# Placing activation tiles against weight tiles in SBUF: new offsets modulo 512 bytes for the squared MLP values, the normed activations and the mixer outputs

## The chip, the cores and the metric

The kernel runs on one core of one Trainium2 chip. The metric is the device time of one execution in microseconds (us); smaller is better. A measurement of a kernel is the median of several runs.

## The reference: what is computed

One layer of a hybrid decoder block on 256 tokens of 2048 features, in float32:

```python
n = rmsnorm(h, g_mix);  z = n @ w_in;  q, k, v, u = split(z)
a = moba_attention(q, k, v, dist_bias)           # 8 heads of 128, one causal block here
c = conformer_conv(u, ...)                       # gate, 31-tap depthwise conv, layernorm, silu
h = h + concat([a, c]) @ w_out
h = h + cross_attention(rmsnorm(h), rmsnorm(mem), wq, wk, wv, wo)
nm = rmsnorm(h, g_mlp)
h = h + square(relu(nm @ w1)) @ w2               # d_ff = 8192
return rmsnorm(h, g_final)
```

The weights are 200 pieces of 1 MiB. Of them 128 belong to the MLP (64 to `w1`, 64 to `w2`).

## The kernel before

**Three matmuls for one.** Every float32 operand of a large product is split in two float32r tiles, a high part H and a low part L, so that a product becomes three matmuls that add into one PSUM bank: high by high, high by low, low by high (`mm3`, line 102, which calls `mm`, line 98; the matmul itself is line 99). Each matmul names a *stationary* operand of 128x128, which a weight load (LDWEIGHTS, on the profile's PEld rows) puts into the array, and a *moving* operand of 128 x N columns, which streams through it. The weight load of the next matmul runs while the present matmul streams.

**The weight steps.** A loop over 200 steps (line 911) handles one 1 MiB piece each. SyncE loads the piece into one of 4 `raw` buffers (line 119, four steps ahead), ScalarE copies its high part into `wh` (line 158) and VectorE subtracts to get the low part `wl` (line 170; in some steps GpSimd, line 168), two steps ahead, into rings of 3 buffers each. TensorE then runs the step's matmuls. The steps are, in order: U 0 to 15, V 16 to 23, QK 24 to 39, MK and MV 40 to 47 (keys and values of the memory), Wout 48 to 63, Wq 64 to 67, Wo 68 to 71, and the MLP from 72: four times 16 steps of W1 and 16 steps of W2. The order of instructions on each engine is the order in which the program is written.

**Two forms of a step.** In `weight_stationary` (line 280; U, QK, MK, Wout, W1; Wq and Wo have the same roles) the weight tiles are stationary and the activations move, 256 columns at a time: 48 matmuls in a step, stationary wh, wh, wl, moving H, L, H. In `act_stationary` (line 293; V, MV, W2) the activations are stationary and the weights move, 512 columns at a time: 24 matmuls in a step, stationary H, H, L, moving wh, wl, wh. Four consecutive steps of a block go through four groups of activations, one group per step.

**The activation tiles.** `act_tiles` holds four groups, each a pair actH, actL of 4 x 256 columns: the normed input of a product (groups 0 to 3, `split_act`, line 181). The eight tiles tagged `mixH`/`mixL` with a0, a1, c0, c1 hold first the mixer outputs (a: attention, c: convolution; they feed Wout), then the cross-attention output (a0, feeds Wo), and in the MLP the squared values sH, sL of block b (`evac_w1`, line 789; they feed W2). For Wo, the tiles of a1 and c0 hold one split piece of weights at their start (`wo_split0`, line 714).

**Where the tiles stand.** `shifted` (line 174) allocates 4*256+32 words and uses 4*256 of them, starting `shift` words in (`ACT_SHIFT`, line 42; `MIX_SHIFT`, line 43). Tiles follow each other in SBUF in the order of first use, so their places depend on the sizes of all before them; the first is the scratch of `dynamic_dma_scratch_size` bytes (line 1017; DMAs here are all issued by SyncE). A row of a stationary operand is 512 bytes and each moving operand is a multiple of 1024, so all parts of one tile have the same byte address modulo 512. In the built program these places are:

| tile | before, address modulo 512 | activation minus weights, modulo 256 (H, L) |
|---|---|---|
| wh, wl (all 6 buffers) | 384 | |
| act group 0: H, L | 192, 320 | (64, 192) |
| act group 1: H, L | 448, 64 | (64, 192) |
| act group 2: H, L | 320, 448 | (192, 64) |
| act group 3: H, L | 64, 192 | (192, 64) |
| a0, also s of block 0: H, L | 0, 128 | (128, 0) |
| a1, also s of block 1: H, L | 256, 384 | (128, 0) |
| c0, also s of block 2: H, L | 256, 0 | (128, 128) |
| c1, also s of block 3: H, L | 384, 128 | (0, 0) |

The last column is worked out from the one before it. It is called the *offset* of a group below.

Of the kernel before, what the change touches and what calls it, by code (L numbers as in the profile page):

```python
# [10 lines left out]
F32R = mybir.dt.float32r  # L11
# [4 lines left out]
P = 128  # L16
T = 256
# [21 lines left out]
WOUT_ORDER = [(0, 0), (1, 0), (2, 0), (0, 1), (1, 1), (2, 1), (3, 0), (3, 1)]  # L39
STEP_US = 5.25  # L40

ACT_SHIFT = (16, 16, 16, 16)
MIX_SHIFT = {"a0": 0, "a1": 0, "c0": 0, "c1": 0}


def bucket(d):
# [29 lines left out]
def tile_hybrid_block(ctx: ExitStack, tc: tile.TileContext, xT, memT, w, par, rel, gfin, out):  # L76
    nc = tc.nc
    act, dve, pool, pe = nc.scalar, Metered(nc.vector), nc.gpsimd, nc.tensor
    ctx.enter_context(tc.manual_schedule())
    sb = ctx.enter_context(tc.tile_pool(name="sb", bufs=1))  # L80
# [4 lines left out]
    def nm(s):  # L85
        count[0] += 1
        return f"{s}_{count[0]}"

    def ring(shape=(P, 512)):
        return sb.tile(list(shape), F32, tag="ring", name=nm("ring"), bufs=7)  # L90
# [81 lines left out]
    act_tiles = {}  # L172

    def shifted(tag, shift, name=None):
        t = sb.tile([P, 4 * T + 32], F32R, tag=tag, name=nm(name or tag))
        return t[:, shift:shift + 4 * T].rearrange("p (a b) -> p a b", a=4)

    def new_act(g):
        act_tiles[g] = tuple(shifted(f"act{x}{g}", ACT_SHIFT[g]) for x in "HL")

    def split_act(g, src, gain, i):
        hi, lo = act_tiles[g]
# [5 lines left out]
    def split_act_group(g, src, gain):  # L188
        new_act(g)
        for i in range(4):  # L190
            split_act(g, src, gain, i)
# [54 lines left out]
    def twice(rb):  # L246
        return rb.unsqueeze(1).to_broadcast([P, 2, T])

    def pair(ap):
        return ap.rearrange("p (a b) -> p a b", a=2)  # L250
# [73 lines left out]
    def split_both(j, g):  # L324
        new_act(g)
        split_tiles(j)
        for i in range(4):
            s = slice(i * 512, (i + 1) * 512)
            split_act(g, hT[g], G_MIX, i)
            act.activation(wh[j][:, s], raw[j][:, s], AF.Copy)  # L330
            dve.tensor_sub(wl[j][:, s], raw[j][:, s], wh[j].bitcast(F32)[:, s])
# [69 lines left out]
    MIX = ["a0", "a1", "c0", "c1"]  # L401
# [35 lines left out]
    mix = {}  # L437

    def mix_tiles(key):
        if key not in mix:  # L440
            mix[key] = tuple(shifted(f"mix{x}{key}", MIX_SHIFT[key]) for x in "HL")
        return mix[key]

    def evac_split(dst, i, src):
# [4 lines left out]
    def self_attention(b):  # L449
# [56 lines left out]
        def evac_o():  # L506
            for h in heads:
                evac_split(mix_tiles(MIX[h // 4]), h % 4, st["o", h])
# [70 lines left out]
    def ln_silu(i):  # L579
        sg, z = ln[i]  # L580
        dve.tensor_tensor(z, z, sg, op=OP.mult)
        hi, lo = mix_tiles(MIX[2 + i // 2])
        s = slice(2 * (i % 2), 2 * (i % 2) + 2)
        act.activation(hi[:, s, :], z, AF.Copy)
        dve.tensor_sub(lo[:, s, :], z, hi.bitcast(F32)[:, s, :])
# [108 lines left out]
    def cx_e(h):  # L694
        if not cx_o:
            mix.clear()
            cx_o.append(mix_tiles("a0"))
        evac_split(cx_o[0], h, cx["o", h])
# [85 lines left out]
    sT = {}  # L784
# [2 lines left out]
    gb = []  # L787

    def evac_w1(b, banks):
        sT[b] = tuple(shifted(f"mix{x}{MIX[b]}", MIX_SHIFT[MIX[b]], f"s{x}{b}") for x in "HL")  # L790
        for n in range(2):
            y, s = ring((P, 2, T)), ring((P, 2, T))
            d = slice(2 * n, 2 * n + 2)
            dve.scalar_tensor_tensor(y, pair(banks[n].ap), 0.0, twice(RB["2"]), op0=OP.max, op1=OP.mult)
            act.activation(s, y, AF.Square)
            act.activation(sT[b][0][:, d, :], y, AF.Square)  # L796
            dve.tensor_sub(sT[b][1][:, d, :], s, sT[b][0].bitcast(F32)[:, d, :])
# [60 lines left out]
    for q in range(4):  # L858
        j0 = MLP0 + 32 * q
        for b in range(4):  # L860
            block(j0 + 4 * b, 4, weight_stationary, act_pair, lambda bk, b=b: evac_w1(b, bk),
                  lag=2 if q == b == 0 else 0)
# [164 lines left out]
```

## Time and profile before

| | us |
|---|---|
| median of 3 runs | 1190.11 (1188.60 to 1190.23) |
| the profiled execution's own time | 1188.36 |
| its span, first to last instruction | 1186.6 |
| TensorE busy in the span | 1160.6 |
| VectorE busy | 707.8 |
| ScalarE busy | 540.8 |
| granted TensorE clock, mean | 0.993 of full speed |

The profile is one execution on the chip. Its engines are PE (matmuls), PEld (weight loads), DVE (VectorE), ACT (ScalarE), POOL (GpSimd) and SP (SyncE, here the DMA queue). A matmul's row gives its start and a duration in which the next one has already begun, since matmuls are pipelined; what a matmul costs is therefore the distance from its start to the start of the next one, here called its *pitch*. Windows are given in us from the start of the span.

### The profile page before, as it was taken

How to read it: one execution, taken by the hardware profiler on the slowest of the kernel's cores; microseconds unless marked ns; L12 is line 12 of the kernel's file. 1: busy time of each engine (PE TensorE's matmuls, PEld its weight loads, DVE VectorE, ACT ScalarE, POOL GpSimd, SP SyncE). 2: the span in 40 equal slices, each digit the busy share in tenths (PEclk: the TensorE clock that was granted, in tenths of full speed). 3: DMA queues.
4: the chain of work that ended last, by engine and by line, in shares of the span. 5: the costliest groups of instructions: out<-in, count | busy, mean ns of one | idle time of the engine just before them, and what ended most of it. 6: DMA issues, size and time to landing. Idle time of an engine off the chain costs nothing.

```text
span 1186.6 us, 18443 instructions
## 1 busy us (share of the span) xinstructions
PE 1160.6 (98%) x7976; PEld 1076.4 (91%) x7976; DVE 707.8 (60%) x821; ACT 540.8 (46%) x564; POOL 113.6 (10%) x100
## 2 busy tenths in 40 slices
PE   7969999999999999999999999999999999999996
PEld 7969899999999999999888999888999888999885
DVE  6659998787666668555444545454455454445443
ACT  7535344465666456554333344333444333444342
POOL 3243121012003003000000000000000000000112
PEclk9989999999999999999999999999999999999999
DMA  9766554444554534545655544555554655554532
GB/s 353 247 195 217 187 205 172 154 145 175 185 190 165 199 115 178 197 159 195 231 183 204 181 178 177 213 178 191 197 180 156 218 194 180 189 199 146 213 139 71
DMA packets 35000, 221.02 MB, mean 186 GB/s; under 512 B 3816, under 2 KB 6504, under 8 KB 9448
## 3 DMA queue, kind: packets, MB, share of 16 engines
q1 hardware_dynamic: 34920, 219.86, 52.5%
q8 instruction: 62, 1.02, 0.3%
q14 instruction: 18, 0.15, 0.0%
HBM read 216.18 MB, written 3.67 MB: 185 GB/s over the span
## 4 chain that ended last, share of the span: by engine, by line
PE 92%; DMA 4%; DVE 2%; ACT 1%; issue 0%; SPq 0%; ACTq 0%; DVEq 0%
PE mm L99 86%; PE cv L99 4%; DMA dram_rev<-ring 3%; PE sm L99 2%; DMA raw<-in_w_dram 1%; DVE wl L65 1%; DVE cv L65 1%; ACT wh L158 0%; PE sm L808 0%; PE sm L494 0%; PE sm L684 0%; SPq L129 0%; SPq L128 0%; DVE acc L65 0%; ACT ring L841 0%
## 5 line engine op out<-in xcount | busy, mean ns | idle before, releaser
L65 DVE TENSOR_TENSOR wl<-raw,wh 128x2048 fp32r<-128x2048 f32 (+1 forms) x205 | 447.0, 2187 | 316.0 <-ACT wh L158 313.4
L158 ACT ACTIVATE wh<-raw 128x2048 fp32r<-128x2048 f32 x195 | 373.5, 1915 | 531.6 <-PE mm L99 421.6
L99 PE MATMUL mm<-actH,wh 128*128 128x256 f32 x1600 | 453.1, 283 | 14.1 <-ACT wh L158 8.0
L99 PE MATMUL mm<-actH,wl 128*128 128x256 f32 x1600 | 450.8, 282 | 1.8 <-DVE wl L65 1.8
L99 PE MATMUL mm<-actL,wh 128*128 128x256 f32 x1600 | 450.3, 281 | 0.0
L99 PEld LDWEIGHTS mm<-actH,wh 128*128 128x128 f32 x1600 | 302.8, 189 | 14.7 <-ACT wh L158 8.2
L99 PEld LDWEIGHTS mm<-actH,wl 128*128 128x128 f32 x1600 | 303.3, 190 | 2.5 <-DVE wl L65 2.5
L99 PEld LDWEIGHTS mm<-actL,wh 128*128 128x128 f32 x1600 | 303.1, 189 | 0.3
L99 PE MATMUL mm<-wh,sL 128*128 128x512 f32 x512 | 202.2, 395 | 0.0
L99 PE MATMUL mm<-wl,sH 128*128 128x512 f32 x512 | 201.4, 393 | 0.0
L99 PE MATMUL mm<-wh,sH 128*128 128x512 f32 x512 | 201.4, 393 | 0.0
L99 PEld LDWEIGHTS mm<-wl,sH 128*128 128x128 f32 x512 | 96.3, 188 | 22.9
L99 PEld LDWEIGHTS mm<-wh,sL 128*128 128x128 f32 x512 | 96.2, 188 | 22.3
L99 PEld LDWEIGHTS mm<-wh,sH 128*128 128x128 f32 x512 | 96.2, 188 | 22.0
L65 DVE SCALAR_TENSOR_TENSOR cv<-hp,part,cv 128x256 f32<-128x256 f32 x240 | 97.7, 479 | 0.0
L892 POOL TENSOR_TENSOR acc<-acc,gb 128x512 f32<-128x512 f32 x6 | 12.1, 2041 | 677.5 <-ACT ring L828 677.5
L65 DVE TENSOR_TENSOR sL<-ring,sH 128x512 fp32r<-128x512 f32 x32 | 22.2, 692 | 67.0 <-ACT sH L796 67.0
L209 POOL TENSOR_TENSOR acc<-acc,ring 128x512 f32<-128x512 f32 x17 | 35.5, 2088 | 168.2 <-ACT ring L208 167.4
L168 POOL TENSOR_TENSOR wl<-raw,wh 128x512 fp32r<-128x512 f32 x24 | 32.4, 1382 | 99.1 <-ACT wh L158 99.1
L99 PE MATMUL mm<-wh,actH 128*128 128x512 f32 x96 | 38.2, 398 | 0.0
L99 PE MATMUL mm<-wh,actL 128*128 128x512 f32 x96 | 37.9, 395 | 0.0
L99 PE MATMUL mm<-wl,actH 128*128 128x512 f32 x96 | 37.9, 394 | 0.0
(156 smaller groups left out, 1042.3 us busy)
## 6 DMA issues: line engine op xcount, KB each, us to landing
raw<-in_w_dram SPq DMA_DIRECT2D x199, 1024.0 KB, 4.8
mem<-in_memT_dram SPq DMA_DIRECT2D x4, 512.0 KB, 7.0
out_dram<-acc SPq DMA_DIRECT2D x8, 256.0 KB, 3.1
hT<-in_xT_dram SPq DMA_DIRECT2D x3, 512.0 KB, 7.4
dram_rev<-ring SPq DMA_DIRECT2D x1, 1532.0 KB
raw<-in_w_dram SPq DMA_DIRECT2D x4, 256.0 KB, 3.9
bias<-dram_rev SPq DMA_DIRECT2D x1, 1024.0 KB, 5.8
gb<-in_gfin_dram SPq DMA_DIRECT2D x4, 256.0 KB, 7.2
```

The costliest lines, as they stand in the source:

```text
L65: return op(out, *args, **kw)
L99: pe.matmul(o, lhsT=lhsT, rhs=rhs, start=not bk.begun, stop=stop, skip_group_check=True)
L158: act.activation(wh[j], raw[j], AF.Copy)
L168: pool.tensor_sub(wl[j][:, s], raw[j][:, s], wh[j].bitcast(F32)[:, s])
L209: eng.tensor_tensor(self.acc, self.acc, sq, op=OP.add)
L892: pool.tensor_mul(d, d, gb[cb])
```

## The change

The room around an activation tile grows from 32 to 128 words, each of the 16 tiles has a shift of its own, and the DMA scratch shrinks from 8192 to 1024 bytes, which moves all tiles. The mixer outputs and the squared values, which share tiles, now differ by 16 words (64 bytes). No instruction is added, removed, resized or moved on any engine; only operand addresses differ.

```diff
-ACT_SHIFT = (16, 16, 16, 16)
-MIX_SHIFT = {"a0": 0, "a1": 0, "c0": 0, "c1": 0}
+ROOM = 128
+ACT_SHIFT = {"H0": 16, "H1": 16, "H2": 112, "H3": 112, "L0": 16, "L1": 16, "L2": 112, "L3": 112}
+S_SHIFT = {"Ha0": 32, "Ha1": 32, "Hc0": 96, "Hc1": 96, "La0": 32, "La1": 32, "Lc0": 96, "Lc1": 96}
+MIX_STEP = 16
...
-        t = sb.tile([P, 4 * T + 32], F32R, tag=tag, name=nm(name or tag))
+        t = sb.tile([P, 4 * T + ROOM], F32R, tag=tag, name=nm(name or tag))
...
-        act_tiles[g] = tuple(shifted(f"act{x}{g}", ACT_SHIFT[g]) for x in "HL")
+        act_tiles[g] = tuple(shifted(f"act{x}{g}", ACT_SHIFT[f"{x}{g}"]) for x in "HL")
...
-            mix[key] = tuple(shifted(f"mix{x}{key}", MIX_SHIFT[key]) for x in "HL")
+            mix[key] = tuple(shifted(f"mix{x}{key}", (S_SHIFT[x + key] + MIX_STEP) % ROOM) for x in "HL")
...
-        sT[b] = tuple(shifted(f"mix{x}{MIX[b]}", MIX_SHIFT[MIX[b]], f"s{x}{b}") for x in "HL")
+        sT[b] = tuple(shifted(f"mix{x}{MIX[b]}", S_SHIFT[x + MIX[b]], f"s{x}{b}") for x in "HL")
...
-    nc = bacc.Bacc("TRN2", target_bir_lowering=False, num_devices=1, dynamic_dma_scratch_size=8192)
+    nc = bacc.Bacc("TRN2", target_bir_lowering=False, num_devices=1, dynamic_dma_scratch_size=1024)
```

The places in the built program after it:

| tile | after, address modulo 512 | offset (H, L) |
|---|---|---|
| wh, wl (all 6 buffers) | 128 | |
| all act groups: H, L | 192, 192 | (64, 64) |
| mixer outputs and cross-attention output: H, L | 192, 192 | (64, 64) |
| squared values s of all blocks: H, L | 128, 128 | (0, 0) |

The one split piece of Wo in a1 and c0 stands at 0 and 256 after the change (before: 256 and 384 in a1, 256 and 0 in c0).

## The prediction

> **What bounds the kernel now.** I read the page first: which engine is busy, and what the chain that ended last is made of.
>
> ```profile
> span 1186.6 us, 18443 instructions
> PE 1160.6 (98%) x7976; PEld 1076.4 (91%) x7976; DVE 707.8 (60%) x821; ACT 540.8 (46%) x564; POOL 113.6 (10%) x100
> PE 92%; DMA 4%; DVE 2%; ACT 1%; issue 0%; SPq 0%; ACTq 0%; DVEq 0%
> ```
>
> TensorE is busy 98% of the span and is 92% of the chain. The next question is where it waits. The view of waits, for TensorE, gives four rows for the first 113.6 us (the two largest below) and none for the rest.
>
> ```profile
> PE mm L99 <- ACT wh L158: 8.0, 1, 8.0
> PE mm L99 <- ACT wh L330: 6.1, 1, 6.1
> ```
>
> So from 113.6 us on, time is the sum of the matmuls' pitches. The busy time of stretches shows it, and shows what the other engines have left (columns: window, its length, then busy us and count of PE, PEld, DVE, ACT, POOL, then granted clock, DMA share, GB/s):
>
> ```profile
> 113.58:158.48 44.90, 44.90 (x197) 36.25 (x195) 44.27 (x81) 20.36 (x18) 8.25 (x8) 1.00 0.53 188
> 158.48:181.00 22.52, 22.52 (x193) 22.52 (x192) 21.53 (x34) 8.82 (x6) 6.57 (x4) 1.00 0.52 191
> 181.00:284.56 103.56, 103.56 (x859) 102.73 (x857) 82.13 (x168) 57.10 (x97) 12.97 (x9) 1.00 0.46 163
> 549.72:638.75 89.03, 89.03 (x386) 72.17 (x385) 43.27 (x27) 32.85 (x20) 0.00 (x0) 1.00 0.57 201
> 638.75:729.06 90.31, 90.31 (x770) 90.30 (x768) 45.57 (x31) 37.24 (x28) 0.00 (x0) 1.00 0.53 187
> 729.06:818.10 89.04, 89.04 (x386) 72.17 (x385) 43.29 (x27) 32.86 (x20) 0.00 (x0) 1.00 0.54 189
> 908.40:997.45 89.05, 89.05 (x387) 72.18 (x385) 43.30 (x27) 32.85 (x20) 0.00 (x0) 1.00 0.54 189
> 1087.75:1176.60 88.85, 88.85 (x386) 71.98 (x384) 41.33 (x38) 35.25 (x37) 13.61 (x8) 1.00 0.37 131
> ```
>
> The rows of 89 us are the four runs of W2 (384 matmuls of 512 columns each), the row of 90.31 is one run of W1 (768 matmuls of 256 columns). PE is busy for the whole of each, at full clock, and in the MLP nothing else exceeds 57%. The exception is 113.58 to 181.00 (V and the first QK block): DVE is busy 44.27 of 44.90 us and 21.53 of 22.52 us there, so matmuls that got shorter would soon wait for `wl`.
>
> **What addresses cost in the trace of before.** The change touches only addresses, and before happens to hold five different offsets, in steps of equal work. I cut windows at the steps of W2, blocks 0 to 3 of one cycle, then at W1, groups 0 to 3, at Wout (a0, a1, c0, c1), and at V, groups 1 and 2.
>
> ```profile
> 571.96:577.57 5.61, 5.61 (x25) 1.00 0.61 197
> 577.57:583.17 5.60, 5.60 (x25) 1.00 0.59 196
> 583.17:588.75 5.58, 5.58 (x25) 1.00 0.53 185
> 588.75:594.23 5.48, 5.48 (x26) 1.00 0.52 187
> ...
> 638.76:644.37 5.61, 5.61 (x49) 1.00 0.53 187
> 644.37:649.99 5.62, 5.62 (x50) 1.00 0.54 191
> 649.99:655.64 5.65, 5.65 (x50) 1.00 0.54 187
> 655.64:661.30 5.66, 5.66 (x51) 1.00 0.53 188
> ...
> 331.38:337.14 5.76, 5.76 (x51) 1.00 0.52 182
> 337.14:342.90 5.76, 5.76 (x51) 1.00 0.61 198
> 354.34:360.04 5.70, 5.70 (x50) 1.00 0.42 171
> 360.04:365.79 5.75, 5.75 (x50) 1.00 0.61 194
> ...
> 119.38:124.94 5.56, 5.56 (x25) 1.00 0.09 12
> 124.94:130.54 5.60, 5.60 (x25) 1.00 0.88 342
> ```
>
> Divided by 24 or 48 matmuls, and set beside the offsets (activation minus weights, modulo 256):
>
> | offset (H, L) | 256 columns move | 512 columns move |
> |---|---|---|
> | (64, 192) | 117.0 ns (W1) | 231.7 (V) |
> | (192, 64) | 117.8 (W1) | 233.3 (V) |
> | (128, 0), both places | 120.0 (Wout) | 233.5 (W2) |
> | (128, 128) | 118.8 (Wout) | 232.5 (W2) |
> | (0, 0) | 119.8 (Wout) | 228.3 (W2) |
>
> Places that are equal modulo 256 but not modulo 512 agree (a0 with a1, groups 0 with 1, blocks 0 with 1), so the pitch goes by the offset modulo 256. The DMA share of these steps lies between 0.09 and 0.88 without a trace in the pitch, so this is TensorE's own: a weight load that reads while the present matmul streams.
>
> Two offsets settle into one pitch. In the W2 step at (0, 0), after the first few matmuls, and in the Wout step at (0, 0), the starts run (first and last shown):
>
> ```profile
> 568.55 0.39 PE L99 MATMUL mm<-wh,sH 128*128 128x512 f32 x1
> 571.27 0.39 PE L99 MATMUL mm<-wh,sH 128*128 128x512 f32 x1
> ...
> 360.39 0.28 PE L99 MATMUL mm<-mixHc,wh 128*128 128x256 f32 x1
> 362.91 0.28 PE L99 MATMUL mm<-mixHc,wh 128*128 128x256 f32 x1
> ```
>
> The first pair spans 12 matmuls: 2.72/12 = 226.7 ns, the least of any W2 step. The second spans 21: 2.52/21 = 120.0 ns, as much as any W1 or Wout step takes. So (0, 0) is the best offset for 512 moving columns and among the worst for 256. The change gives W2 the first and moves everything with 256 columns to (64, 64), which no step of before has.
>
> [...]
>
> **The change part by part.**
>
> *Squared values to (0, 0).* 4 x 16 steps of W2 take 89.03 + 89.04 + 89.05 + 88.85 = 355.97 us. At 226.7 ns they take 4 x 16 x 24 x 0.2267 = 348.2: **7.8 us** less. In before, L of the best step stands 256 off, not 0; since places 256 apart agree, I take it as the same. All of it is on the path: DVE and ACT are busy under half of these windows and the weights come in at about 200 GB/s, where one row above shows 342. The lower bound is 0.
>
> *Normed activations to (64, 64), 256 columns moving.* There are 104 such steps. I leave out U (steps 0 to 15, in and next to the waits for ACT) and the first QK block (DVE full): 84 steps, 4032 matmuls, at 90.31 us / 768 = 117.6 ns. The new pitch has to be bounded. From above: where before has a mixture and both its parts, the mixture is no faster than the slower part ((128, 0): 120.0 against 118.8 and 119.8; with 512 columns 233.5 against 232.5 and 228.3). By that, (64, 64) takes at most the 117.0 of (64, 192). From below: half of the stall-free 226.7 for half the columns, 113.3. I take the middle, 115.2: 4032 x 2.4 = **9.7 us**. The ends are 17.3 and 2.4; if the inference from mixtures fails, the far ends are those of other offsets, 120.0, a loss of 9.7.
>
> *Mixer and cross-attention outputs to (64, 64).* 16 steps of Wout and 4 of Wo, 960 matmuls, at about 119.5 (between 118.8 and 120.0). To 115.2: 960 x 4.3 = **4.1 us** (5.9 to 2.4; at 120.0 a loss of 0.5).
>
> *V and MV to (64, 64), 512 columns moving.* V gains nothing, since DVE is full there. MV has 96 matmuls at about 232.5: to 229.5, between 226.7 and the 231.7 of (64, 192): **0.3 us**.
>
> *Other engines.* VectorE's, ScalarE's and DMA work is the same; its tiles move too. The row for writing sL covers four places modulo 512 and is flat at 691 to 694 ns, so I cost this at nothing:
>
> ```profile
> L65 DVE TENSOR_TENSOR sL<-ring,sH x32: 691/693/694, 492.8 to 1093.3; 128x512 fp32r<-128x512 f32 x32
> ```
>
> The smaller DMA scratch is cost at nothing as well, since every DMA is issued by SyncE's queue. If TensorE shortens by this much, what is late next is `wl` in the first 181 us, already left out. The start and the tail of 10 us stay.
>
> Sum: 7.8 + 9.7 + 4.1 + 0.3 = 21.9 us. The profiled execution took 1188.4 us (span 1186.6), below all three runs shown; against it 1166.5, against the median of 1190.1 **1168 us**.
>
> **The rivals.**
>
> - *(64, 64) is stall-free as (0, 0) is with 512 columns.* Uniform offsets are what settled in the rows above, and 113.3 may be where this one does. 7.8 + 17.3 + 5.9 + 0.6 = 31.6: 1158 us. Against it: with 256 columns a weight load has to fit beside half the streaming time, and no step of before averages under 117.0.
> - *Only W2 gains.* (64, 64) is no better than the mixture it replaces: 117.0 to 118 in the acts. 7.8, about 2 from the mixer outputs, and 0 to 2 from the acts: 1178 to 1181 us.
> - *The other side: every matmul of 256 columns collides.* (64, 64) locks as (0, 0) did in Wout, on every matmul. At 120.0 the acts lose 9.7 and the mixer outputs 0.5, against 7.8 from W2: 1192.5. It decides from a pitch of 119.6 upward; at 122 it is 18 + 2.4 - 7.8 = 13 us: 1203.
> - *Addresses do nothing* and the differences of steps have another cause that follows the groups (such as the order in a block): 1190. Against it: the same offsets agree across three kinds of steps. [...]
>
> **How the numbers follow.** A measurement of this kernel can tell about 0.2% (2.4 us) from no change. Chances: the forecast (pitch of 114 to 117) 0.42; stall-free 0.25; only W2 0.20; collides 0.09 (of which a third within 0.2%); nothing 0.04. So faster 0.87, same 0.07, slower 0.06. The range leaves out the collision, the null case and a little at either end: from 1155 (stall-free, with 3 us beyond it) to 1185 (only W2, with the acts 1 ns worse).
>
> **What would show it.** In the profile after: W2 windows of 87.0 us with starts 226.7 ns apart in all four blocks; W1 windows of 88.5 us (115.2) without the difference between blocks and groups, against 87.0 if stall-free, 90.3 if unchanged and 92.2 if locked at 120; Wout steps equal to W1 steps. Wrong would be a W2 step still at 5.6 us, equal times for groups but no gain, or a new wait of PE for `wh` or `wl` after 181 us.

## The result, and the profile after

| | before | after |
|---|---|---|
| median of 4 runs, us | 1189.59 (1188.60 to 1190.23) | 1179.61 (1176.69 to 1180.83) |
| the profiled execution, us | 1188.36 | 1176.69 |
| its span, us | 1186.6 | 1174.9 |

The ratio of the times is 0.991, with a 95% interval of 0.989 to 0.993: faster, by about half of what was predicted. The page of the changed kernel shows the same picture as before with a shorter TensorE:

```profile
span 1174.9 us, 18443 instructions
PE 1149.1 (98%) x7976; PEld 1072.3 (91%) x7976; DVE 707.3 (60%) x821; ACT 540.9 (46%) x564; POOL 116.4 (10%) x100
PE 92%; DMA 4%; ACT 1%; DVE 1%; SPq 0%; issue 0%; ACTq 0%
```

The waits of TensorE are the old ones at the start. The third row, for `wl`, is one of the four rows of before too, with the same 1.8 us in two waits:

```profile
PE mm L101 <- ACT wh L160: 7.8, 1, 7.8
PE mm L101 <- ACT wh L332: 6.4, 2, 6.0
PE mm L101 <- DVE wl L67: 1.8, 2, 1.5
```

After the start a single wait of 0.2 us is left, ahead of a small matmul of the cross-attention. So again time is the sum of pitches. The busy time of stretches of the changed kernel follows: QK and MK; Wout; Wq and Wo; the first W1 run; a W2 run, a W1 run, and the last W2 run up to the start of its last matmul; then single steps: a W1 step of the first run and one of the second, a W2 step, a Wout step (columns: window, its length, then busy us and count of PE, granted clock, DMA share, GB/s).

```profile
158.71:283.41 124.70, 124.70 (x1049) 1.00 0.48 170
306.68:397.81 91.13, 91.13 (x776) 1.00 0.53 186
397.81:451.71 53.90, 53.68 (x439) 1.00 0.44 155
451.71:545.44 93.73, 93.73 (x809) 1.00 0.51 181
545.44:632.50 87.06, 87.06 (x386) 1.00 0.58 205
632.50:722.96 90.46, 90.46 (x769) 1.00 0.52 187
...
1078.03:1164.88 86.85, 86.85 (x386) 1.00 0.37 134
...
457.15:462.59 5.44, 5.44 (x51) 1.00 0.49 184
638.16:643.82 5.66, 5.66 (x51) 1.00 0.49 182
567.23:572.66 5.43, 5.43 (x25) 1.00 0.53 198
...
324.31:329.97 5.66, 5.66 (x51) 1.00 0.46 179
```

Three stretches of before that the prediction does not show (QK and MK, Wout, the first W1 run), in the same form:

```profile
158.48:284.56 126.08, 126.08 (x1050) 1.00 0.47 168
307.75:400.18 92.43, 92.43 (x775) 1.00 0.52 183
...
455.21:549.72 94.51, 94.51 (x809) 1.00 0.50 179
```

Row against row, the 11.7 us that the span lost come from these places:

| stretch | before | after | change, us |
|---|---|---|---|
| four W2 runs | 89.03, 89.04, 89.05, 88.82 | 87.06, 87.08, 87.07, 86.85 | -7.9 |
| QK, MK | 126.08 | 124.70 | -1.4 |
| Wout | 92.43 | 91.13 | -1.3 |
| Wq, Wo | 55.03 | 53.90 | -1.1 |
| first W1 run | 94.51 | 93.73 | -0.8 |
| three later W1 runs | 90.31, 90.30, 90.30 | 90.46 each | +0.5 |
| start, V, MV | 113.58 + 44.90 + 23.19 | 113.69 + 45.02 + 23.27 | +0.3 |

Two thirds of the gain is W2. Each of its steps now takes 5.44 us (24 x 226.7 ns; the windows are cut at hundredths, so rows say 5.43 to 5.45), without a difference between blocks. A W1 step of the second run takes 5.65 us or 117.8 ns a matmul, which is what before had. The first four steps of the first run take 5.44 us at the same offset, 113.3 ns, and so do the two steps of Wo ahead of them; further on in that run other matmuls stand between, and its last two steps take 5.65 again. **The same offset, (64, 64), has two settled pitches, 113.3 and 117.8, and most steps got the slower one.**

Before had a sign of this. Its W1 groups 0 and 1, at (64, 192), take 5.61 and 5.62 us in the first cycle of four steps, the rows that the prediction used. In the second cycle they take this:

```profile
661.30:666.95 5.65, 5.65 (x51) 1.00 0.42 173
666.95:672.60 5.65, 5.65 (x50) 1.00 0.28 80
```

The third cycle is at 5.62 and 5.61 again and the fourth at 5.65. So one placement already had more than one pitch there.

### The profile page after: what moved, and what is told of

Read it like the earlier page. It is cut to its first block, busy times and chain, and to the rows that moved or that the text cites. A ratio compares the mean times of both kernels' runs of the same rounds, so it can differ in the third digit from the quotient of the medians.

```text
span 1174.9 us, 18443 instructions
## 1 busy us (share of the span) xinstructions
PE 1149.1 (98%) x7976; PEld 1072.3 (91%) x7976; DVE 707.3 (60%) x821; ACT 540.9 (46%) x564; POOL 116.4 (10%) x100
## 4 chain that ended last, share of the span: by engine, by line
PE 92%; DMA 4%; ACT 1%; DVE 1%; SPq 0%; issue 0%; ACTq 0%
PE mm L101 87%; PE cv L101 3%; DMA dram_rev<-ring 3%; PE sm L101 2%; DMA raw<-in_w_dram 1%; DVE wl L67 1%; ACT wh L160 1%; PE sm L810 0%; PE sm L496 0%; PE sm L686 0%; DVE small L67 0%; SPq L131 0%; SPq L130 0%; ACT actH L186 0%; ACT L676 0%
## 5 line engine op out<-in xcount | busy, mean ns | idle before, releaser
L101 PE MATMUL mm<-wh,sL 128*128 128x512 f32 x512 | 199.2, 389 | 0.0
```

Of the source, the lines that this page charges most:

```text
L101: pe.matmul(o, lhsT=lhsT, rhs=rhs, start=not bk.begun, stop=stop, skip_group_check=True)
```

## The experiments

All edits are against the changed kernel and change only addresses, except in the run with three extra matmuls. The tables' numbers are shifts in words within a tile; the offsets that they give are named in the text. "Uniform" means H and L at the same offset. In the edits `MIX_SHIFT` takes the place of `S_SHIFT` plus `MIX_STEP` for the mixer and cross-attention outputs; the line that reads it, and tables that follow the same pattern, are left out.

### The two parts alone

Squared values alone at their new place; everything else at the offsets of before:

```diff
-ACT_SHIFT = {"H0": 16, "H1": 16, "H2": 112, "H3": 112, "L0": 16, "L1": 16, "L2": 112, "L3": 112}
+ACT_SHIFT = {"H0": 80, "H1": 16, "H2": 80, "H3": 16, "L0": 112, "L1": 48, "L2": 112, "L3": 48}
-MIX_STEP = 16
+MIX_SHIFT = {"Ha0": 64, "Ha1": 0, "Hc0": 64, "Hc1": 96, "La0": 96, "La1": 32, "Lc0": 0, "Lc1": 32}
```

> The changed kernel with the offsets of before for acts, mixer outputs and cross-attention output; only the squared values stay at (0, 0). Offset theory: W2 windows of 87.0 us, W1 windows of 90.3, Wout steps of 5.70 to 5.76: 7.8 us below before, 1181.8. Rival, the gain comes from something else that the change moved (scratch, places of other tiles): a time like the changed kernel's, or before's.

Measured: 1182.22 us (1181.10 to 1184.29), ratio 0.994 (0.993 to 0.995). Busy time of PE in that run, a W2 run, a W1 step and a Wout step:

```profile
550.39:637.52 87.13, 87.13 (x386) 1.00 0.58 205
...
648.76:654.41 5.65, 5.65 (x51) 1.00 0.51 187
332.05:337.81 5.76, 5.76 (x50) 1.00 0.52 182
```

W2 has its whole gain, and W1 and Wout are as before. The other half, with activations, mixer and cross-attention outputs at (64, 64) and the squared values where before had them:

```diff
-S_SHIFT = {"Ha0": 32, "Ha1": 32, "Hc0": 96, "Hc1": 96, "La0": 32, "La1": 32, "Lc0": 96, "Lc1": 96}
+S_SHIFT = {"Ha0": 64, "Ha1": 0, "Hc0": 64, "Hc1": 96, "La0": 96, "La1": 32, "Lc0": 0, "Lc1": 32}
```

> The other half of the change alone: normed activations, mixer and cross-attention outputs at (64, 64), squared values at the offsets of before. Offset theory: W2 windows of 89.0 us as before, the rest as in the changed kernel. With s_only 7.4 us below before and the changed kernel 10.0 below, 2 to 4 us below before: 1186 to 1188. Rival, the parts do not add, since the phase that W2 leaves decides the pitch of W1 after it: over 5 us off that.

Measured: 1185.08 us (1184.90 to 1185.71), ratio 0.996 (0.995 to 0.997). A W2 run, one of its steps (block 3), and a W1 run:

```profile
545.80:634.85 89.05, 89.05 (x387) 1.00 0.56 200
562.58:568.05 5.47, 5.47 (x25) 1.00 0.89 345
...
634.85:725.30 90.45, 90.45 (x769) 1.00 0.53 187
```

The median is a little below the 1186 to 1188 expected. W2 is back at its old 89.05 us, and W1 stays at 90.45, as in the changed kernel. The spans of the two halves, 1179.3 and 1183.1, lie 7.3 and 3.5 us below that of before, 10.8 together against 11.7 for the whole change. V starts at 114.26 and 113.74 us in them, 113.58 before; with that difference of the start taken out they are 8.0 and 3.7. The two parts of this change simply add.

### Only the offset counts

All tiles, weights too, 64 bytes further, and the L tiles another 256 bytes away from the H tiles:

```diff
-ACT_SHIFT = {"H0": 16, "H1": 16, "H2": 112, "H3": 112, "L0": 16, "L1": 16, "L2": 112, "L3": 112}
+ACT_SHIFT = {"H0": 16, "H1": 16, "H2": 112, "H3": 112, "L0": 80, "L1": 80, "L2": 48, "L3": 48}
...
-dynamic_dma_scratch_size=1024
+dynamic_dma_scratch_size=1088
```

> The changed kernel with every tile 64 bytes further on (a DMA scratch of 1088 bytes), and all L tiles of acts, mixer outputs and squared values another 256 bytes further: offsets (64, 320) and (0, 256). Theory that only the offset modulo 256 counts: the changed kernel's profile again, W2 windows 87.0 us, W1 117.8 or 113.3 ns, 1177 to 1181 us. Rival, places count absolutely or modulo 512: W2 steps leave 226.7 ns, for instance to 233 (89.6 us a window, 10 us in all).

Measured: 1179.01 us (1178.68 to 1179.93), ratio 0.991 (0.990 to 0.992), the changed kernel's. A W1 step of the first run and one of the second:

```profile
465.85:471.29 5.44, 5.44 (x50) 1.00 0.55 193
641.42:647.08 5.66, 5.66 (x51) 1.00 0.53 185
```

Both take what they take in the changed kernel, 5.44 and 5.66 us, the first at 113.3 ns and the second at 117.8. Moving everything by 64 bytes, and H against L by 256, changes nothing that these rows or the time (1179.01 against 1179.61 us) show.

### A map of uniform offsets

Three kernels place the four groups at four offsets each: 0, 128, 192 and 32 (squared values 64, 128, 192, 32); 96, 160, 224 and 16; 208, 176, 240 and 48. The first one's table:

```diff
-ACT_SHIFT = {"H0": 16, "H1": 16, "H2": 112, "H3": 112, "L0": 16, "L1": 16, "L2": 112, "L3": 112}
+ACT_SHIFT = {"H0": 0, "H1": 32, "H2": 16, "H3": 104, "L0": 0, "L1": 32, "L2": 16, "L3": 104}
```

> One uniform offset per group or block, in bytes behind the weights: acts of groups 0 to 3 and mixer outputs of a0, a1, c0, c1 at 0, 128, 192, 32; squared values of blocks 0 to 3 at 64, 128, 192, 32. Offset theory (the pitch goes by the offset modulo 256 between moving and stationary operand): W1 groups 0 and 1 take 5.76 us (120.0 ns) and 5.70 (118.7); W2 block 0 takes 5.60 us (233.3 ns, as V in the changed kernel) and block 1 5.58 (232.4). 192 and 32 are open: 113.3 to 120 and 226.7 to 235. Rival, the order in the block decides and not the place: all W1 groups keep 5.62 to 5.66 us and W2 blocks 5.44.

> As scan_a, with offsets 96, 160, 224, 16 for the four groups of acts, mixer outputs and squared values. Offset theory: if only the 64-byte part of the offset counts, 96, 160, 224 and 16 repeat 64, 128, 192 and 0 (117.8 or 113.3, 118.7, the value of 192, and 120.0 ns for 256 columns; 233.3, 232.4, the value of 192, and 226.7 for 512). If it is finer, they lie elsewhere. Rival, the order in the block decides: no difference from the changed kernel.

> A map, for want of a rule: activations, mixer outputs and squared values at the uniform offsets 208, 176, 240 and 48 bytes for groups and blocks 0 to 3 (H and L alike). A 256-column step is 48 matmuls, a 512-column step 24. Seen so far for 256 columns: 160 gives 5.70 us a step, 192 gives 5.44 or 5.65 by its two settled pitches, 224 gives 5.67, 32 gives 5.60, 64 gives 5.44 or 5.65. If the good offset is a narrow place at 192, then 208 and 176 give 5.60 to 5.70 in the W1 runs and only places at multiples of 64 bytes hold 113.3 ns. If it is the bottom of a broad dip, 176 and 208 lie between 5.44 and 5.65 and may have one settled pitch only. 512 columns: 0 and 16 gave 226.7 ns, 192 gave 229.5, 224 gave 233.3; 208 and 240 should then lie between 229 and 233.5, 176 near 231, 48 near 233.4. The whole kernel: 1180 to 1195.

One run each took 1186.52, 1194.81 and 1188.57 us. W1 steps of the first kernel, groups 0 to 3, and a V step at offset 0:

```profile
637.39:643.14 5.75, 5.75 (x50) 1.00 0.53 184
643.14:648.84 5.70, 5.70 (x51) 1.00 0.59 191
648.84:654.30 5.46, 5.46 (x50) 1.00 0.55 188
654.30:659.90 5.60, 5.60 (x50) 1.00 0.52 186
...
137.09:142.54 5.45, 5.45 (x25) 1.00 0.55 192
```

From the second, the W1 step at 96 and the W2 step at 16:

```profile
642.51:648.28 5.77, 5.77 (x50) 1.00 0.66 203
614.81:620.25 5.44, 5.44 (x25) 1.00 0.51 188
```

From the third, the W1 step at 176 and the W2 step at 240:

```profile
689.92:695.64 5.72, 5.72 (x50) 1.00 0.31 96
...
605.60:611.08 5.48, 5.48 (x25) 1.00 0.51 187
```

All offsets seen, as us of a step divided by its 48 or 24 matmuls:

| offset | 256 columns, ns | 512 columns, ns | | offset | 256 columns, ns | 512 columns, ns |
|---|---|---|---|---|---|---|
| 0 | 120 | 226.7 | | 128 | 119 | 232 |
| 16 | 119 | 226.7 | | 160 | 117 or 119 | 234 |
| 32 | 116.7 | 233 | | 176 | 119 | 230 |
| 48 | 118 | 233 | | 192 | **113.3** or 117.8 | 229 |
| 64 | **113.3** or 117.8 | 233 | | 208 | 117 or 119 | 232 |
| 96 | 120 | 234 | | 224 | 118 | 233 |
| | | | | 240 | 117 | 228 |

The order of the groups does not set the pitch: the offset does, in steps finer than 64 bytes, for each of the two forms in its own way. The DMA share of the rows above runs from 0.31 to 0.66 beside it without effect. Offset 192 is the place that the change missed: about 113.3 with 256 columns like 64, but 229 instead of 233 with 512. It is a narrow place: 176 gives 119, 5.72 us a step, slower than the 5.60 to 5.70 that were expected, and 208 takes 5.72 or 5.60. Two pitches are not peculiar to 64 and 192: in the later W1 runs the steps at 208 change between 5.72 and 5.60 us from one cycle of four steps to the next, and those at 160 between 5.70 and 5.63. No simple rule in the offset is to be seen in the table.

### Which two reads collide

If a matmul is held up by the weight load of the *next* matmul, its pitch should depend on the place of its moving tile against the next stationary one. The next edit keeps those distances uniform while the distance within a matmul's own pair becomes a mixture: starting from the placement of the next section (activations at 192, squared values at 0), `wl` and the L tiles both move 64 bytes.

```diff
+        t = sb.tile([P, 2048 + ROOM], F32R, tag="wl", name=f"wl{j}", bufs=SPLIT_BUFS)
+        wl[j] = t[:, 16:2064]
```

> all192, with the low weights wl 64 bytes further on, and with them the L tiles of acts, mixer outputs and squared values. While a matmul with moving H streams, wh is loaded for the next; while L streams, wl is loaded. So each matmul's moving operand keeps its offset to the weights loaded for the NEXT matmul (192, and 0 in W2), while to the weights it is multiplied with itself the offsets become 192, 0, 128 (0, -64, 64 in W2). Theory that the collision is with the next load: pitches as in all192, 113.3 and 226.7 ns. Rival, the matmul's own pair counts: mixed offsets, 118 to 120 ns in W1 (90.5 to 92 us a window) and about 233 in W2 (89.5).

Measured: 1190.66 us in one run. A W1 and a W2 step:

```profile
656.83:662.52 5.69, 5.69 (x50) 1.00 0.50 183
567.67:573.22 5.55, 5.55 (x26) 1.00 1.00 357
```

118.5 and 231.1 ns, instead of 113.3 or 117.8 and 226.7. The simple form of the collision with the next weight load falls. The traces show the weight load of the next matmul, 0.19 us long, starting together with the present matmul (both at 639.93 us in before). That it holds the matmul up, as the prediction reads it, is not shown. What takes its place is not settled. In this run the distances within a matmul's own pair are a mixture, and the place also jumps from one matmul to the next. The jumps alone can't be it: in the map above there are none, and the pitch still goes by the offset. But whether the own pair counts, or the next load together with the jumps, this run can't tell, since its edit brings both.

### A better place

Activations, mixer and cross-attention outputs at 192, squared values at 0:

```diff
+ACT_SHIFT = {"H0": 48, "H1": 48, "H2": 16, "H3": 16, "L0": 48, "L1": 48, "L2": 16, "L3": 16}
+MIX_SHIFT = {"Ha0": 80, "Ha1": 80, "Hc0": 16, "Hc1": 16, "La0": 80, "La1": 80, "Lc0": 16, "Lc1": 16}
```

> The changed kernel with normed activations, mixer outputs and cross-attention output 192 bytes behind the weights in place of 64; squared values stay at 0. From scan_a, where the steps at 192 took 5.46 us each (113.3 ns after the first few matmuls): W1 windows of 87.1 to 87.4 us in place of 90.5, Wout steps of 5.44 to 5.46 in place of 5.65, 15 to 17 us below the changed kernel, 1162 to 1165. Rival, the weights or VectorE become the bound once TensorE runs this fast everywhere: TensorE waits for wh or wl, and less than half of that is left, over 1171.

Measured: 1170.93 us (1169.72 to 1171.81), ratio 0.984 (0.983 to 0.986). A QK step, a Wout step, a W1 step of the first run, one of the second, that whole run, and V:

```profile
168.63:174.07 5.44, 5.44 (x50) 1.00 1.00 420
325.84:331.50 5.66, 5.66 (x51) 1.00 0.52 185
458.63:464.07 5.44, 5.44 (x50) 1.00 0.55 193
637.65:643.30 5.65, 5.65 (x51) 1.00 0.51 186
626.34:716.79 90.45, 90.45 (x769) 1.00 0.53 188
113.55:157.74 44.19, 44.19 (x197) 1.00 0.53 191
```

Faster than the changed kernel, but above the 1162 to 1165 expected. The rival, waits for `wh` or `wl`, is not the reason: from V on TensorE waits for nothing in this trace. Offset 192 has the two settled pitches too: the undisturbed steps of QK and of the first W1 run get 113.3, Wout and the later W1 runs 117.8, 90.45 us a run again.

### What picks one of the two pitches

One extra matmul of 260, 264 or 268 columns ahead of W1 runs 2, 3 and 4 of the changed kernel (extra work whose result is not used) shifts the run by 0.12 to 0.13 us:

```diff
+    for q in (1, 2, 3):
+        at("mid", MLP0 + 32 * q, lambda q=q: kick(MLP0 + 32 * q, 256 + 4 * q))
```

> The changed kernel with one extra matmul ahead of the second, third and fourth run of W1, of 260, 264 and 268 columns into an unused bank (its result is used nowhere). All addresses stay. Theory that (64, 64) has two stable pitches, 117.8 and 113.3 ns, and that the phase at entry picks one: at least one of the three windows falls from 90.5 to about 87.2 us. Rival, the place in the program picks it (what other engines do there): all three windows stay at 90.5 plus 0.1 for the extra matmul.

Measured: 1177.96 us in one run; the first W1 step of each of the three runs stays at 117.8 ns, of which one row:

```profile
811.22:816.87 5.65, 5.65 (x50) 1.00 0.52 186
```

None of the three shifts moved it. They are nearly alike, so this is a weak test of the phase at entry. Next, from the kernel with everything at 192: the squared values of block 3, whose step is the last ahead of each later W1 run, also at 192, and the mixer outputs of block 1 at 128.

```diff
-S_SHIFT = {"Ha0": 32, "Ha1": 32, "Hc0": 96, "Hc1": 96, "La0": 32, "La1": 32, "Lc0": 96, "Lc1": 96}
+S_SHIFT = {"Ha0": 32, "Ha1": 32, "Hc0": 96, "Hc1": 16, "La0": 32, "La1": 32, "Lc0": 96, "Lc1": 16}
...
+MIX_SHIFT = {"Ha0": 80, "Ha1": 64, "Hc0": 16, "Hc1": 16, "La0": 80, "La1": 64, "Lc0": 16, "Lc1": 16}
```

> Against the kernel with everything at 192 and the squared values at 0 (1170.9 us), two edits: the squared values of block 3, whose W2 step is the last before each later W1 run, stand at 192 instead of 0, and the mixer outputs of block 1 at 128. Theory (which of its two settled pitches an offset takes is set by the pitch of the matmuls just before it and is then kept; a step at 192 that follows 512-column matmuls at 192, or a step at 128, has always come in at 113.3): the three later W1 runs take 16 x 5.44 = 87.0 us each instead of 90.45, 10.2 less; the 16 W2 steps of block 3 take 5.50 instead of 5.44, 0.9 more; in Wout 12 of 16 steps fall from 5.65 to 5.45 and 4 rise to 5.70, 2.2 less. Sum 1170.9 - 10.2 + 0.9 - 2.2 = 1159.4, range 1158 to 1161. Rival (the settled pitch depends on something else, such as what the DMA queues or other engines do in that stretch): W1 runs 2 to 4 stay at 117.8, 90.45 us each, and the kernel is at 1169.5 to 1172.

Measured: 1170.16 us (1169.05 to 1171.60), ratio 0.983 (0.981 to 0.984). A Wout step at 128, the one behind it at 192, a later one at 192, and a W1 step of the second run:

```profile
320.08:325.78 5.70, 5.70 (x50) 1.00 0.50 174
325.78:331.25 5.47, 5.47 (x50) 1.00 0.55 192
342.43:347.87 5.44, 5.44 (x51) 1.00 0.67 211
...
630.24:635.90 5.66, 5.66 (x51) 1.00 0.50 178
```

Half of the theory holds. In Wout, which stood at 117.8 throughout with every tile at 192, each step at 192 behind a step at 128 comes in at 113.3 and the later ones stay there; the block takes 88.96 us, against 91.13 at 117.8 in the changed kernel. The W1 runs behind 512-column matmuls at 192 stay at 117.8, so the forecast of 1159.4 us failed and the time is the rival's.

The last step of U adds something to this. In this kernel and in the one with everything at 192 it stands at 192, and the matmuls ahead of it have the same operands. It takes 5.44 us in the trace of the kernel with everything at 192 (first row) and 5.65 in this one (second row):

```profile
108.11:113.55 5.44, 5.44 (x51) 1.00 0.66 233
107.86:113.51 5.65, 5.65 (x50) 1.00 0.64 226
```

The two traces part in the step before, where TensorE waits for VectorE, 1.2 us in the one and 0.3 in the other, and at the first matmuls behind that wait. So the same addresses with the same matmuls ahead can settle at either pitch, here in two executions on two chips that differ in time.

The last kernel therefore leads with 256-column matmuls: group 0 and the mixer outputs of block 1 at 32, all else at 192, squared values at 0.

```diff
+ACT_SHIFT = {"H0": 8, "H1": 48, "H2": 16, "H3": 16, "L0": 8, "L1": 48, "L2": 16, "L3": 16}
+MIX_SHIFT = {"Ha0": 80, "Ha1": 40, "Hc0": 16, "Hc1": 16, "La0": 80, "La1": 40, "Lc0": 16, "Lc1": 16}
```

> Activations of group 0 and the mixer outputs of block 1 at offset 32, all other activations and mixer outputs at 192, squared values all at 0. Theory (offset 192 has two settled pitches, and the matmuls ahead decide which; every step at 192 that followed 256-column matmuls at 128 or 32 so far came in at 113.3 ns and stayed there): in the three later W1 runs every first of four steps takes 5.60 us and the three behind it 5.45, 87.8 us a run instead of 90.45, 8.0 less in all. Against the kernel that led Wout with offset 128 (1170.2 us): squared values back at 0 0.9 less, four Wout steps 5.60 for 5.70 0.3 less, the 9 other 256-column steps of group 0 5.60 for 5.44 1.3 more, its 3 512-column steps 0.3 more. Sum 1162.6, range 1161 to 1164. Rival (in the stretches of the later W1 runs something other than the matmuls ahead holds 192 at 117.8): the three steps stay at 5.65, 90.2 us a run, and the kernel is at 1169 to 1171.

Measured: **1164.28 us** (1164.21 to 1167.25), ratio 0.979 (0.978 to 0.981), the fastest version. The second W1 run, first two steps, fifth, sixth and eighth step, and the whole run:

```profile
626.36:631.97 5.61, 5.61 (x50) 1.00 0.64 200
631.97:637.62 5.65, 5.65 (x51) 1.00 0.53 186
...
648.92:654.53 5.61, 5.61 (x51) 1.00 0.39 164
654.53:659.98 5.45, 5.45 (x50) 1.00 0.23 69
...
665.42:670.86 5.44, 5.44 (x50) 1.00 0.50 190
...
626.36:714.74 88.38, 88.38 (x769) 1.00 0.55 192
```

The runs fall from 90.45 to 88.38 us, not to 87.8: the first cycle of four steps stays at 117.8, and from the second on the steps at 192 are at 113.3. That is 3 x 0.6 = 1.8 us over the three runs and accounts for the 1.7 us above the expected 1162.6. The steps at 32 ahead of the two cycles have the same pitch, 116.7 ns, and yet lead to different ones. So the matmuls ahead have a part in it, but not by their pitch alone. With the last step of U above, some phase at entry (how the starts of the matmuls lie in time) is the likely rest, but it is not shown. Another rival has no run: the outputs of a cycle go to two of four PSUM banks, and those of the next cycle to the other two, the rhythm in which 160, 208 and the (64, 192) of before change. The bank alone doesn't decide here, since the first and the third cycle write the same two and are at 117.8 and 113.3.

## Why the prediction was half right

The time, 1179.6 us, lies in the stated range of 1155 to 1185, and the change went the way that was forecast. The mechanism of the forecast is right for W2 alone. For the other two large terms a pitch of 114 to 117 was expected, and no settled stretch of the changed kernel has one. That the range holds the result is due to its upper end, which was set for the rival in which only W2 gains.

**What bounds the kernel: right.** No new wait for `wh` or `wl` appeared, and TensorE's chain share stayed at 92%. The 1.8 us of waits for `wl` were there before, and the rows for writing sL stay at 692 to 694 ns.

**Squared values: right.** Predicted 7.8 us, 7.9 in the windows, 7.4 between the medians of the kernel with this part alone. Taking (0, 0) with L 256 bytes away as the same offset was right too: with the 256 bytes added the kernel took 1179.0 us against 1179.6, where W2 at 233 ns would have cost 10 us, as an estimate from the W2 windows.

**Activations: the step that failed.** It was the upper bound of the new pitch: "By that, (64, 64) takes at most the 117.0 of (64, 192)", from the rule that a mixture is no faster than its slower part. (64, 64) settles at 117.8 in most steps, above that bound, so the two mixtures in which before had W1 (117.0 and 117.8) were as good as the uniform place. The bound rested on two cases in which the rule happened to hold, and on one cycle of W1: in the next cycle (64, 192) itself takes 5.65 us, 117.7 ns. Of 9.7 us came 1.8: 1.4 in QK and MK, 0.8 in the first W1 run and 0.1 in Wq, less 0.5 lost in the later runs.

**The middle between two bounds was no pitch at all.** Where the step is undisturbed, (64, 64) gives 113.3 or 117.8, the one at the lower bound and the other above the upper, and 115.2 in no settled stretch. The lower bound, half of 226.7, turned out to be a pitch that exists, in the stretches of 5.44 us.

**Mixer and cross-attention outputs: same error.** Wout went from 118.8 to 120.0 down to 117.8, not to 115.2: 1.3 us there. Wo gave 1.0 of the 1.1 us of Wq and Wo, since its last two steps went from 5.76 to 5.44. Together that is 2.3 of 4.1.

**V and MV: the sign.** V and MV at (64, 64) take 233.3 ns and lose 0.1 us each. That VectorE hides V was too careful: with offset 192 the V stretch falls to 44.2 us from 44.9 and QK steps run at 113.3 without a wait. This is why leaving out the first QK block was also unneeded.

**The rivals.** "Only W2 gains", at 1178 to 1181, is what happened, at a measured 1179.6, part by part: 7.8, about 2 and 0 to 2 us there, 7.9, 2.3 and 1.8 in the windows. It had a chance of 0.20, the forecast 0.42. "Stall-free" came true in some steps and is what the better placement buys. "Every matmul collides" did not occur: uniform 0 and 96 do give 120 ns, but not 64. "Addresses do nothing" is refuted by the squared values alone: in the run that moved only them, W2 steps went from 5.60 to 5.44 us by place alone.

**The median.** The profiled execution lies 2.9 us below the median of its runs. In the profiles, the start of V, which ends the stretch in which TensorE waits for ScalarE, lies between 113.5 and 114.3 us where the rows above give it, and in the run of everything 64 bytes further the two W1 steps start 3.26 us later than in the changed kernel (465.85 and 641.42 against 462.59 and 638.16 us) at the same pitch. A spread of this size is probably that; the other executions have no profile to show it.

## What to carry to other kernels

When TensorE is the bound and its matmuls run back to back, compare the pitch of equal steps whose tiles stand at different addresses; places were worth 2% here without an instruction changed (ratio 0.979 in the last kernel). Measure a place before building on it, for each number of moving columns by itself, and look at two stretches of it: a pitch may have more than one settled value (113.3 and 117.8 ns at 64 and at 192), and a value between two bounds may not exist (115.2 ns at 64). Shift tiles one kind at a time. In the change the two halves added (10.8 of 11.7 us); in the last kernels they did not, since a new place for one group changed the pitch of the groups behind it (steps at 192 from 5.65 to 5.44 us).

## What was not expected of the hardware

- One placement, with equal instructions, settles at 113.3 or at 117.8 ns for 256 columns and keeps that, 117.8 for whole runs of 768 matmuls and 113.3 for six steps in a row, 288 matmuls. The matmuls ahead have a part in the choice: in steps that no other matmuls interrupt, 128 always led 192 into 113.3, 32 in all but the first cycle of a later W1 run; a step of 512 columns at 192 led to 113.3 ahead of QK and to 117.8 ahead of W1, and one extra matmul changed nothing. The same matmuls ahead led to either in the last step of U.
- The best place for 512 moving columns (0 and 16: 226.7 ns) is among the worst for 256 (120 and 119 ns).
- The least pitches seen are 226.7 ns for 512 columns and 113.3 for 256, one half as far as the traces resolve it (5.44 us for a step of 24 and for one of 48).
